# A two-layer hybrid trunk on one core: key weights split in small buffers, values of linear attention kept in SBUF, other orders of additions, loads and first steps

## The chip, the cores and the metric

The kernel runs on one core of one Trainium2 chip. The metric is device time in microseconds (us) of one execution. Engines are named as in the profile: PE (TensorE, matrix products), DVE (VectorE), ACT (ScalarE), POOL (GpSimd), and SP, which issues all DMAs.

## The reference

The input is 1024 positions of width 1024 in float32. Two layers follow, each a token mixer and an MLP, with an RMSNorm ahead of every part and the input added to its output. Layer 0 mixes with dilated attention, which the change leaves alone. Layer 1 mixes with gated linear attention: four heads, keys of 128, values of 256, in chunks of 64 positions. Cut to what matters:

```python
proj = h @ w_in                               # q, k, v, g_out, gate_lr
gk = gate_lr @ w_gate_up + b_gate
log_a = log_sigmoid(gk) / 16.0
b = cumsum(log_a)                             # within a chunk
q_t, k_t = q * exp(b), k * exp(-b)
o_intra = (causal(q_t @ k_t.T)) @ v
U = (k * exp(b_last - b)).T @ v               # state is a * state + U
o = o_intra + q_t @ s_prev
o = rmsnorm(o, norm_w) * silu(g_out)
x = x + o @ w_out
a = relu(h @ w_up)                            # the MLP of each layer
x = x + (a * a) @ w_down
```

## The kernel before, in words

All engines run in an order written out by the program: what Python calls first stands first in an engine's queue, and nothing is reordered. Large products are made with fp32r, three passes for a product of full precision (high by high, high by low, low by high), so every operand is first cut on ACT into a high part and subtracted on DVE to get the low part. They use a scheme of seven block products for eight, so weights and results are also added and subtracted on DVE.

**The MLP of layer 0** (`Up.run`, L786) goes over 16 column pairs p, each of seven products s of 12 matmuls. ACT copies a bank of PSUM to a small tile e (`copy`, L719), DVE adds another bank to it (`done`, L726, and `add`, L747), ACT squares, and SP stores. Beside it, for p from 4 on, runs `Ahead` (L527): it splits the weights of the linear attention's queries and keys (`w_in`, four heads), to be stored and fetched again later. A step of it, at each odd s, issues first the subtractions left over from the step before, then its own cuts: `load` brings four blocks in two tiles, the step after cuts two of them, and five more follow. Pairs of high and low tiles come from the ring k4 (25 tiles of 512 KB).

**The keys' stage** (`finish_keys`, L435) makes queries and keys from these weights, again by seven products a head, with banks X, V, Y, Z; sums of them (L1781) go out to memory as qks. Work of the gates (`Gate`, L1827: logits, log sigmoid, a scan over positions, exponentials, four products that scale queries and keys, a store) is entered in an agenda by clock, and `advance` runs what is due after each product.

**The gate products** (`Values`, L833) make silu's input and the values: 28 steps n of 24 matmuls, two column groups g. `step` (L954) first copies or adds the banks that are complete (`sums`, L933), then makes the operands for step n+2 (`total`, L865; `rounded`, L887; `remain`, L895, with dl at L898), loads for n+5, and issues the product; `advance` comes after it, with `Silu` (L1902) and the late gates. Both groups are stored in memory: silu's input as zscr, the values as uscr.

**The linear attention** (`Pair`, L1964) runs after the last step, two heads at a time. `load_keys` and `wide` load the keys, the gates (G) and the values (V) back; `scores` (L1993) makes masked scores AM; `turn` transposes keys through a bank and ACT copies them (L2008); `update` (L2010) adds to the state Sb; `output` (L2027) makes pO, ACT squares it into gj (L2037); `scaled`, one tick later, takes the root (L208 to L214) and multiplies by G into y (L2045). The first three blocks of the first pair run before the output projection, the rest, as a list of steps, between the products of that projection (`add_block`, L192 to L194), whose weights are prepared by `Weights` (L134 load, L148 high part on ACT, L149 low part on DVE), called raw, whi and wlo.

Rings of tiles: h8 (12), k4 (25), t2 (8 tiles of 256 KB), r6 (1); PSUM has eight banks, taken in turn. A new tile waits until the tile that last had its place is no longer read.

Of the kernel before, what the change touches and what calls it, by code (L numbers as in the profile page):

```python
# [41 lines left out]
def hybrid_trunk(ctx, tc, x, norm_mix, norm_mlp, norm_fin, a_in, a_out, g_in, g_up, g_b, g_nw,  # L42
# [68 lines left out]
    class Weights:  # L111
        def __init__(self):
            self.slots = []
            self.scales = []
            self.ndma = 0
            self.nprep = 0
            self.used = 0
            self.freed = 0
            self.limit = 5
            self.second = pool  # L120
            self.parts = {}
            self.raws = {}
# [29 lines left out]
        def pump(self):  # L152
            while self.ndma < min(self.nprep + RAW, len(self.slots)):
# [107 lines left out]
    class Halves:  # L261
# [173 lines left out]
        def finish_keys(self, low_rank):  # L435
# [8 lines left out]
            def go(p, s):  # L444
                up.product(p, s)
                advance()

            go(0, P1)
# [5 lines left out]
            up.fetch(0, "b")  # L454
# [5 lines left out]
            up.fetch(1, "b")  # L460
# [9 lines left out]
            go(3, P2)  # L470
            up.add(2, P2)
# [3 lines left out]
            up.fetch(0, "g", "d")  # L475
            go(0, P6)
            self.sum3()
# [3 lines left out]
            up.fetch(1, "g", "d")  # L481
# [3 lines left out]
            up.fetch(2, "b")  # L485
            go(1, P5)
            go(0, P7)
# [4 lines left out]
            up.fetch(2, "g", "d")  # L492
# [4 lines left out]
            up.fetch(3, "b")  # L497
# [3 lines left out]
            up.done(2, P6)  # L501
            go(2, P5)
            go(0, P3)
            up.add(0, P3)
            up.fetch(3, "g", "d")
# [100 lines left out]

    def up_columns(i):
# [12 lines left out]
    class Up:  # L620
# [4 lines left out]
        def __init__(self, i):  # L625
# [5 lines left out]
            self.side = Ahead(key_columns, raw_k4, wpre[2]) if i == 0 else None  # L631
# [154 lines left out]
        def run(self, tail):  # L786
# [7 lines left out]
            for p in range(3, NP):  # L794
                first = 2 if p == 3 else 0
                for s in range(first, 7):
# [13 lines left out]
                    if self.side is not None and 4 <= p < NP - 1 and s % 2:  # L810
                        self.side.step()
# [147 lines left out]


# [516 lines left out]
    def out_proj(layer, wbc_row, o, up):  # L1477
# [26 lines left out]
        for tb in range(NB):  # L1504
# [3 lines left out]
            if tb == (NB - 4 if layer else 3):  # L1508
                W.limit = 6
            for n in range(2):  # L1510
# [316 lines left out]
    class Gate:  # L1827
# [10 lines left out]
        def first(self):  # L1838
            z = logits(self.h, self.half) if self.z is None else self.z
            b = bgate[:, self.h:self.h + 1]  # L1840
            a = self.a = t2([P, 512], F32, "ga")
            m = self.m = t2([P, 512], F32, "gmn")
# [35 lines left out]
        def keys(self):  # L1878
            bs = lambda t: t.rearrange("p (b s) -> p b s", s=P)
            d = [self.d[:, c, :].unsqueeze(2).to_broadcast([P, 4, CH]) for c in range(2)]  # L1880
            mm, sk = k4([P, 2, 512], F32, "qkm"), k4([P, 2, 512], F32, "qsk")
            q, k, eq, ek, es = (bs(t) for t in (self.qk[:, 0, :], self.qk[:, 1, :], self.eb[:, 0, :], self.eb[:, 1, :],
                                                self.es))
            q_m, k_m, q_s, kd = (bs(t[:, i, :]) for t in (mm, sk) for i in range(2))
            dve.scalar_tensor_tensor(q_m, q, DK ** -0.5, eq, op0=OP.mult, op1=OP.mult)
            pool.tensor_tensor(q_s[:, :, CH:], q_m[:, :, CH:], d[0], op=OP.mult)
            dve.tensor_tensor(k_m, k, ek, op=OP.mult)
            to = gks[self.h][:, :, 512 * self.half:512 * self.half + 512]
            sp.dma_start(to[:, 0:2, :], mm)
            dve.scalar_tensor_tensor(q_s[:, :, :CH], q[:, :, :CH], DK ** -0.5, es[:, :, :CH], op0=OP.mult, op1=OP.mult)  # L1890
            dve.tensor_tensor(kd[:, :, CH:], k[:, :, CH:], es[:, :, CH:], op=OP.mult)
            dve.tensor_tensor(kd[:, :, :CH], k_m[:, :, :CH], d[1], op=OP.mult)
            sp.dma_start(to[:, 2:4, :], sk)

        def plan(self, t, gap):
# [4 lines left out]
            at(t + 3 * gap - (gap > 1), self.keys, 8)  # L1900

    class Silu:  # L1902
# [19 lines left out]
        def third(self):  # L1922
# [4 lines left out]
            sp.dma_start(self.at(gscr), e)  # L1927

        def plan(self, t):
            for n, (fn, rank) in enumerate(((self.load, 9), (self.first, 8), (self.second, 8), (self.third, 8))):  # L1930
                at(t + n + (n > 0), fn, rank)

    gates = Values(g_in, [2048, 1024], lambda g: (zscr, uscr)[g])
    gates.h = keys.h
    c = clock[0]
    zg = {}

    def early_logits(h, half):
        if h not in zg:
            zg[h] = k4([P, S], F32, "zg")  # L1940
        act.activation(zg[h][:, 512 * half:512 * half + 512], logits(h, half), AF.Copy)

    def late_gate(h, half, t):
        def fn():
            Gate(h, half, zg[h][:, 512 * half:512 * half + 512]).plan(t, 1)
        at(t - 1, fn)

    for n, (h, half) in enumerate(((0, 1), (1, 1), (0, 0), (1, 0))):
        Gate(h, half).plan(c + 15 + 3 * n, 2)
    for n, (h, half) in enumerate(((2, 1), (3, 1), (2, 0), (3, 0))):  # L1950
        at(c + 25 + n // 2, lambda h=h, half=half: early_logits(h, half), 9)
        late_gate(h, half, c + 30 + 2 * n)
    for n in range(5):
        at(c + 17 + n, lambda n=n: gates.load(n), 9)
    at(c + 22, lambda: gates.prep(0), 9)
    at(c + 25, lambda: gates.prep(1), 9)
    halves.finish_keys(low_rank)
    c = clock[0]
    for n, (i, q) in enumerate(((0, 0), (1, 0), (0, 1), (2, 0), (3, 0), (1, 1), (2, 1), (3, 1))):
        Silu(i, q).plan(c + (7, 9, 13, 15, 17, 19, 21, 23)[n])  # L1960

    AM = [k4([P, NB, P], F32, "AM") for _ in range(2)]

    class Pair:  # L1964


        def __init__(self, h0):
            self.h0 = h0
            self.st = {}
            self.y = {}  # L1970
            self.Sb = [None, None]

        def load_keys(self):
            self.q_m, self.k_m, self.q_s, self.kT = [[k4([P, NB, P], F32, n) for _ in range(2)]
                                                     for n in ("q_m", "k_m", "q_s", "kT")]
            for i, ts in ((0, self.k_m), (1, self.q_m)):
                for j in range(2):
                    sp.dma_start(ts[j], gks[self.h0 + j][:, 1 - i, :].rearrange("p (b s) -> p b s", s=P))
            for i, ts in ((3, self.kT), (2, self.q_s)):
# [3 lines left out]
        def wide(self, name, src, half):  # L1983
            ts = getattr(self, name, None)
            if ts is None:
                ts = [h8([P, NB, DV], F32, name) for _ in range(2)]
                setattr(self, name, ts)
            for j in range(2):
                c = DV * (self.h0 + j)
                sp.dma_start(ts[j][:, 4 * half:4 * half + 4, :],  # L1990
                             src[512 * half:512 * half + 512, c:c + DV].rearrange("(b p) c -> p b c", p=P))
# [18 lines left out]
        def update(self, b):  # L2010
            if b == NB - 1:
                return
            ps = bank("pU").rearrange("p (i d) -> p i d", i=2)
            for i in range(2):
                pe.matmul(ps[:, i, :], self.kd[i][:, b, :], self.V[i][:, b, :], start=True, stop=True)  # L2015
            if b % 4 == 0:
                self.Sb = [k4([P, 4, DV], F32, "Sb") for _ in range(2)]
            for i in range(2):
                new = self.Sb[i][:, b % 4, :]
# [7 lines left out]
        def output(self, b):  # L2027
            po = bank("pO").rearrange("p (i d) -> p i d", i=2)
            ss = sm([P, 2], "gss")
            for i in range(2):  # L2030
                if b:
                    pe.matmul(po[:, i, :], self.q_s[i][:, b, :], self.st.pop((b, i)), start=True, stop=False,  # L2032
                              skip_group_check=True)
                pe.matmul(po[:, i, :], AM[i][:, b, :], self.V[i][:, b, :], start=b == 0, stop=True,  # L2034
                          skip_group_check=True)
                junk = t2([P, DV], F32, "gj")
                act.activation(junk, po[:, i, :], AF.Square, accum_out=ss[:, i:i + 1])  # L2037
# [148 lines left out]
```

## Time and profile before

| what | value |
|---|---|
| median of 3 runs | 2707.7 us (2706.05 to 2709.4) |
| profiled execution, its time | 2707.54 us |
| its span | 2705.8 us |
| PE busy | 2609.8 us |
| DVE busy | 1877.5 us |
| ACT busy | 1281.4 us |
| bytes moved | 536.43 MB |

The span runs from the first to the last instruction on the core; 1.7 us of the time lie around it. A row of the time line gives start, length, engine, line, operation, names out<-in, and in brackets the idle time of the engine before it with what ended it. "PEclk" in a window is the mean clock that PE was granted, as a share of full. Matmuls overlap, so the length of one is more than the distance to the next.

### The profile page before, as it was taken

To read this page: it belongs to the slowest core of one execution; us is meant where nothing else is said; L and a number is where in the kernel's file an instruction comes from. 1 tells how busy PE (TensorE), PEld (TensorE's weight loads), DVE (VectorE), ACT (ScalarE), POOL (GpSimd) and SP (SyncE) were. 2 spreads that over 40 slices of the span, in tenths; PEclk is the share of its full clock that TensorE was granted. 3 is DMA by queue.
4 is the path that set the end of the run, shared out by engine and by line. 5 is a ranking of instruction groups with operands and counts; after the bars stand their busy time and mean duration, and the time that the engine had idled before them with its cause. 6 is when DMAs were issued, how large, how long until landed. Compare 5 with 4: busy or idle time off the path is not lost. (4 is left out here: it accounts for less than half of the span.)

```text
span 2705.8 us, 33577 instructions
## 1 busy us (share of the span) xinstructions
PE 2609.8 (96%) x12096; PEld 2159.5 (80%) x12096; DVE 1877.5 (69%) x3002; ACT 1281.4 (47%) x2344; POOL 34.7 (1%) x40
## 2 busy tenths in 40 slices
PE   8999999999999999898999999999689999999998
PEld 6888888888888887776888888777578888888887
DVE  7766788888888565666668775677455666656567
ACT  6443455555555354454544443454234555453344
POOL 0000000000000000000000000310000000000000
PEclk9999999999999999999999999999899999999999
DMA  5775456556556557666788755777534644486543
GB/s 183 247 269 175 124 140 161 144 146 165 135 153 196 181 198 251 203 218 210 271 299 304 257 204 187 256 246 237 217 109 156 242 158 145 152 315 214 191 146 126
DMA packets 355832, 536.43 MB, mean 198 GB/s; under 512 B 23408, under 2 KB 187632, under 8 KB 355664
## 3 DMA queue, kind: packets, MB, share of 16 engines
q1 hardware_dynamic: 355664, 534.27, 60.4%
q8 instruction: 95, 1.56, 0.2%
q14 instruction: 73, 0.60, 0.1%
HBM read 335.29 MB, written 173.74 MB: 188 GB/s over the span
## 5 line engine op out<-in xcount | busy, mean ns | idle before, releaser
L1607 PE MATMUL pB<-dh 128*128 128x512 f32 x512 | 199.2, 389 | 0.0
L1607 PE MATMUL pB<-dl,dh 128*128 128x512 f32 x512 | 199.2, 389 | 0.0
L1607 PE MATMUL pB<-dh,dl 128*128 128x512 f32 x512 | 199.2, 389 | 0.0
L201 DVE TENSOR_TENSOR dl<-sin,dh 128x1024 fp32r<-128x1024 f32 x112 | 136.7, 1221 | 65.6 <-ACT dh L198 62.6
L714 PE MATMUL pV<-s4h,wd 128*128 128x512 f32 x480 | 165.7, 408 | 13.4 <-DVE rb L739 8.6
L198 ACT ACTIVATE dh<-sin 128x1024 fp32r<-128x1024 f32 x112 | 117.8, 1052 | 80.6 <-PE pB L1607 26.7
L1021 ACT ACTIVATE pt<-pt,orow 128x128 f32<-128x128 f32 (+1 forms) x192 | 85.0, 443 | 146.4 <-DVE orow L1019 144.4
L1607 PE MATMUL pA<-dh 128*128 128x512 f32 x384 | 149.6, 389 | 0.0
L1607 PE MATMUL pA<-dh,dl 128*128 128x512 f32 x384 | 149.4, 389 | 0.0
L1607 PE MATMUL pA<-dl,dh 128*128 128x512 f32 x384 | 149.4, 389 | 0.0
L198 ACT ACTIVATE dh<-kept 128x1024 fp32r<-128x1024 f32 x64 | 67.8, 1060 | 146.2 <-DVE kept L1572 105.2
L714 PEld LDWEIGHTS pV<-s4h,wd 128*128 128x128 f32 x480 | 92.8, 193 | 34.9 <-DVE rb L739 9.5
L1607 PEld LDWEIGHTS pB<-dl,dh 128*128 128x128 f32 x512 | 96.1, 188 | 20.0
L1607 PEld LDWEIGHTS pB<-dh 128*128 128x128 f32 x512 | 96.1, 188 | 19.9
L1607 PEld LDWEIGHTS pB<-dh,dl 128*128 128x128 f32 x512 | 96.1, 188 | 19.9
L719 ACT ACTIVATE e<-pX 128x512 f32<-128x512 f32 x108 | 63.6, 589 | 101.1 <-PE pX L714 101.1
L714 PE MATMUL pX<-s2h,wbh 128*128 128x512 f32 x240 | 97.7, 407 | 9.8 <-ACT e L719 9.8
L714 PE MATMUL pX<-s3h,wgh 128*128 128x512 f32 x240 | 98.6, 411 | 7.9 <-ACT e L719 7.9
L652 DVE TENSOR_TENSOR wbl<-t,wbh 128x1024 fp32r<-128x1024 f32 x48 | 58.8, 1225 | 66.8 <-ACT wbh L651 66.8
L723 ACT ACTIVATE c<-c 128x512 f32<-128x512 f32 x64 | 40.4, 631 | 123.4 <-DVE c L751 73.5
L652 DVE TENSOR_TENSOR wal<-raw,wah 128x512 fp32r<-128x512 f32 x96 | 65.9, 687 | 44.8 <-ACT wah L651 44.8
L714 PE MATMUL pX<-a11h,wah 128*128 128x512 f32 x240 | 95.9, 399 | 0.0
(321 smaller groups left out, 7436.8 us busy)
## 6 DMA issues: line engine op xcount, KB each, us to landing
sin<-acts SPq DMA_DIRECT2D x112, 512.0 KB, 4.6
acts<-s SPq DMA_DIRECT2D x64, 512.0 KB, 3.5
raw<-in_mlp_w_down_dram SPq DMA_DIRECT2D x64, 512.0 KB, 5.0
raw<-in_attn_w_in_dram SPq DMA_DIRECT2D x96, 256.0 KB, 4.4
cw<-c SPq DMA_DIRECT2D x192, 128.0 KB, 2.3
raw<-in_mlp_w_up_dram SPq DMA_DIRECT2D x48, 512.0 KB, 6.0
acts<-c SPq DMA_DIRECT2D x64, 256.0 KB, 2.2
kept<-in_mlp_w_down_dram SPq DMA_DIRECT2D x32, 512.0 KB, 6.7
```

What stands on the lines that cost most here:

```text
L198: act.activation(hi, src, AF.Copy)
L201: dve.tensor_tensor(lo, src, hi.bitcast(F32), op=OP.subtract)
L652: self.remain(lambda: dve.tensor_tensor(lo, src, hi.bitcast(F32), op=OP.subtract))
L714: pe.matmul(st[b], u[:, k, :], v, start=first and k + n == 0, stop=k == 3 and n == 2, skip_group_check=True)
L719: act.activation(e, self.st[p]["X"], AF.Copy)
L723: act.activation(r, r, AF.Relu)
L1021: act.activation(pt[:, i, :128 * n], pt[:, i, :128 * n], AF.Exp, scale=-1.0, bias=m, accum_out=self.row[:, r, HD:HD + 1])
L1607: pe.matmul(self.acc[s][t], a[:, k, c], b[:, k, :], start=fresh and m + k + v == 0, stop=m == 7 and k == 1 and v == 2, skip_group_check=True)
```

## The change

There are four parts. **Small buffers:** `Trickle` takes the place of `Ahead`. It cuts one block into a pair of small tiles th and tl (ring t2) at a time, and stores each by itself, so that 14 stores of half the size stand for 7. Its raw blocks lie in the tile of r6 and one of t2. A step without work stands behind the load, and the steps come where p + s is even. **Keys:** the agenda is run ahead of a product, not behind it; fetches of split weights stand at other products; a gate's two tiles are one of k4, its four products are made in place on DVE alone, and their store comes one clock later. All late gates take their logits in the gate stage, not from a copy. **Gate products:** `Gates.paced` makes the total of step n+2 first, then the sums, then the high part, then runs the agenda, then makes the low part and the product. **Linear attention:** values are added straight into four SBUF tiles V; uscr and its loads are gone. Keys and gates are loaded, and scores, turn and the first block run, by the agenda between the steps 19 to 27; the last product is in two halves with a block behind each. The root is taken behind each block's output, the rest of the scaling (`flush`) behind the next block's update. The output weights' raw loads begin at steps 24 and 25 of the agenda, and later ones wait until the last block of the projection's first round.

```diff
-                    if self.side is not None and 4 <= p < NP - 1 and s % 2:
+                    if self.side is not None and 4 <= p < NP - 1 and (p + s) % 2 == 0:
                         self.side.step()
...
+            def load():
+                t = wk.tile([P, 3, 4, DK], F32, name="traw", tag="r6", bufs=1)
+                x = t2([P, 4, DK], F32, "traw1")
...
+            def cut(src, hi, lo, i, j):
+                h, l = t2([P, 4, DK], F32R, "th"), t2([P, 4, DK], F32R, "tl")
+                act.activation(h, r[src], AF.Copy)
+                def rest():
+                    dve.tensor_tensor(l, r[src], h.bitcast(F32), op=OP.subtract)
+                    for t, n, k in ((h, hi, i), (l, lo, j)):
+                        sp.dma_start(...)
+                self.behind.append(rest)
...
+            self.todo.extend((load, lambda: None,
+                              lambda: cut("b11", "ah", "al", 0, 0),
+                              lambda: cut("b21", "ah", "al", 1, 1),
+                              lambda: cut("b22", "d", "d", 0, 1),
+                              three, four, five, lambda: cut("b21", "gh", "gl", 1, 1)))
...
             def go(p, s):
+                advance()
                 up.product(p, s)
-                advance()
...
+        def paced(self, n, between, blocks=range(4)):
+            self.load(n + 5)
+            ahead = n + 2 < self.STEPS
+            if ahead and n + 2 not in self.t:
+                self.total(n + 2)
+            self.sums(n)
+            if ahead:
+                self.rounded(n + 2)
+            between()
+            if ahead:
+                self.remain(n + 2)
+            self.product(n, blocks)
...
+            half, quad = divmod({"c11": 0, "c12": 1, "c21": 2, "c22": 3}[name], 2)
+            if (quad, half) not in self.V:
+                self.V[quad, half] = h8([P, 4, 512], F32, "V")
+            dve.tensor_tensor(self.V[quad, half][:, t, :], self.acc[s][t], c, op=OP.add)
...
         def step(self, b):
-            self.output(b)
-            self.update(b + 1) if b + 1 < NB else None
+            po, ss = self.output(b)
+            self.update(b + 1)
+            self.flush()
+            self.open = b, po, self.root(ss)
...
+    for t, fn in ((19, lambda: one.load_keys(("k_m", "q_m", "kT"), Pair.joined)),
+                  (20, lambda: one.load_keys(("q_s",), Pair.apart)),
+                  (20, clear_scores),
+                  (22, lambda: one.load_gates(0)),
+                  (23, lambda: one.load_gates(1)),
+                  (23, out_weights),
+                  (24, lambda: (W.dma(), W.dma())),
+                  (25, lambda: (W.dma(), W.dma())),
+                  (24, lambda: one.scores(0)),
+                  (25, lambda: (one.turn(0), one.scores(1))),
+                  (26, lambda: one.turn(1)),
+                  (27, begin)):
+        at(c + t, fn, 9)
+    for n in range(gates.STEPS - 1):
+        gates.paced(n, advance)
...
+    for p in range(2):
+        blocks = [2 * p, 2 * p + 1]
+        if p == 0:
+            gates.paced(last, advance, blocks)
+        else:
+            gates.product(last, blocks)
+        for t in blocks:
+            gates.add("c21", "B", t, 1)
+        one.step(p + 1)
+        W.prep(dve)
```

More of the change, by code (lines that the diff above doesn't have):

```diff
@@ L1950, in hybrid_trunk @@
[L1950 to L1952 removed]
+        Gate(h, half).plan(c + 16 + 3 * n, 2)
     for n in range(5):
[L1954 to L1956 removed]
+        at(c + 18 + n, lambda n=n: gates.load(n), 9)
+    at(c + 23, lambda: gates.prep(0), 9)
+    at(c + 26, lambda: gates.prep(1), 9)
@@ L2078, in hybrid_trunk, with clear_scores, out_weights @@
-    for t in range(4):
-        gates.add("c21", "B", t, 1)
-    keys.h.clear()
-    one.wide("V", uscr, 1)
-    ol = []
-    W.second = dve
-    W.limit = 2
-    one.start()
-    tick()
-    for b in range(3):
-        one.step(b)
-        tick()
+    def clear_scores():
+        for _ in range(2):
+            t = k4([P, NB, P], F32, "AM")
+            pool.memset(t, 0.0)
+            AM.append(t)
+    def out_weights():
+        for k in range(0, KT, 2):
+            add_rows(g_out, k, gnw)
```

251 lines of the change are left out of this document (134 added, 117 removed).

## Prediction

> **What bounds the kernel now.** I read the busy times of the engines first, then what PE waited for, then the stretches that the change touches, each as one window. Times are microseconds; a difference of 0.2% (5.4 us) is about what a measurement of this kernel can tell from no change.
>
> ```profile
> PE 2609.8 (96%) x12096; PEld 2159.5 (80%) x12096; DVE 1877.5 (69%) x3002; ACT 1281.4 (47%) x2344; POOL 34.7 (1%) x40
> ```
>
> PE is the bound, and neither the number of its products nor their shapes change, so the time can only move by what PE loses to waits and to a lower clock. The waits of PE, by what they waited for (sum, times, longest):
>
> ```profile
> PE pX L714 <- ACT e L719: 17.7, 14, 3.6
> PE pO L2034 <- ACT gj L2037: 15.0, 2, 14.4
> PE pO L2032 <- ACT gj L2037: 11.7, 14, 1.7
> PE pV L714 <- DVE rb L739: 8.6, 2, 5.9
> PE pB L913 <- DVE c L928: 5.1, 1, 5.1
> PE pV L714 <- DVE qk L1781: 3.7, 2, 3.0
> PE pA L1998 <- DVE c L928: 2.9, 1, 2.9
> ```
>
> All seven lie in stages that the change rewrites. The windows put sizes to them. The first is ten column pairs of layer 0's MLP beside the splitting of the keys' weights, the second the same ten of layer 1, without it; then come the keys, the gate products, and linear attention's start and rest. The columns are length, busy PE (count), PEld, DVE, ACT, POOL, PEclk, DMA share, GB/s.
>
> ```profile
> 1056.18:1284.39 228.21, 204.07 (x841) 162.50 (x840) 145.50 (x214) 113.13 (x169) 0.00 (x0) 0.96 0.62 210
> 2160.01:2350.41 190.40, 190.40 (x841) 157.50 (x840) 119.68 (x171) 96.76 (x140) 0.00 (x0) 1.00 0.47 155
> 1630.00:1730.00 100.00, 93.78 (x418) 75.56 (x418) 59.74 (x99) 47.60 (x89) 14.04 (x15) 0.98 0.66 234
> 1790.00:1830.00 40.00, 34.86 (x142) 28.31 (x141) 32.93 (x38) 18.08 (x22) 0.94 (x1) 0.91 0.77 266
> 1888.00:1928.00 40.00, 19.95 (x100) 16.37 (x99) 17.24 (x39) 9.61 (x28) 0.00 (x0) 0.79 0.82 313
> 1928.00:2045.00 117.00, 103.85 (x473) 82.78 (x474) 59.79 (x153) 32.64 (x104) 0.00 (x0) 0.96 0.31 103
> ```
>
> The same 841 matmuls take 37.8 longer in layer 0. One matmul there comes every 190.40/841 = 0.226, a product of 12 every 2.72, a gate step of 24 every 5.43. For the others, idle time plus the share below full clock: keys 6.2 + 2.0 = 8.2; gates 5.1 + 3.6 = 8.7; start 20.1 plus some 3.4 of half clock while PE worked (an estimate: much of the lower clock fell on idle time) = 23.5; rest 13.2 + 4.7 = 17.9. In all 96.
>
> **Splitting the keys' weights.** The work stays: 28 cuts on ACT, 28 subtractions and 16 differences on DVE. Its place changes; here is ACT in that stage, where th, ah and gh are cuts and e the copy that a later product waits for. Before:
>
> ```order
> L719 ACTIVATE e_10000<-pX 128x512
> L651 ACTIVATE wbh<-t 128x1024
> L719 ACTIVATE e_10042<-pX 128x512
> L651 ACTIVATE wgh<-t 128x1024
> L560 ACTIVATE ah<-praw 128x512 x2
> L723 ACTIVATE rb<-rb 128x1024
> ```
>
> Now:
>
> ```order
> L705 ACTIVATE wah<-raw 128x512
> L629 ACTIVATE th<-traw_10469 128x512
> L773 ACTIVATE e_10623<-pX 128x512
> L705 ACTIVATE wah<-raw 128x512
> L777 ACTIVATE c_10639<-c_10639 128x512
> L778 ACTIVATE c_10639<-c_10639 128x512
> L629 ACTIVATE th<-traw 128x512
> L773 ACTIVATE e_10666<-pX 128x512
> ```
>
> The two cuts in a row, one step behind their load, become single cuts, each in front of an e, with an empty step behind the load. What the load costs now, and what a clean column pair leaves of room:
>
> ```profile
> 1117.67 2.69 SPq L548 DMA_DIRECT2D praw<-in_gla_w_in_dram  x4
> 1122.14 0.63 ACT L560 ACTIVATE ah<-praw 128x512 fp32r<-128x512 f32 x1 [2.62 <-DMA praw<-in_gla_w_in_dram]
> 1125.12 0.63 ACT L560 ACTIVATE ah<-praw 128x512 fp32r<-128x512 f32 x1 [2.35 <-DMA praw<-in_gla_w_in_dram]
> 1131.39 0.58 ACT L719 ACTIVATE e<-pX 128x512 f32<-128x512 f32 x1
> 1132.02 0.79 PE L714 MATMUL pX<-s2h,wbh 128*128 128x512 f32 x1 [3.62 <-ACT e L719]
> 1288.76 0.58 ACT L719 ACTIVATE e<-pX 128x512 f32<-128x512 f32 x1
> 1289.83 0.39 PE L714 MATMUL pX<-s2h,wbh 128*128 128x512 f32 x1
> ```
>
> ACT stood 2.62 + 2.35 before two cuts, all behind them slid, and PE waited 3.62. The four places with the largest such waits, as windows:
>
> ```profile
> 1072.00:1084.00 12.00, 9.28 (x34) 7.16 (x33) 5.01 (x7) 6.83 (x10) 0.00 (x0) 0.86 0.49 169
> 1128.00:1140.00 12.00, 8.38 (x26) 6.38 (x25) 8.24 (x14) 6.31 (x11) 0.00 (x0) 0.72 0.57 177
> 1195.00:1207.00 12.00, 10.05 (x37) 7.78 (x36) 8.58 (x14) 6.60 (x11) 0.00 (x0) 0.86 0.65 223
> 1231.00:1247.00 16.00, 10.11 (x33) 7.87 (x32) 5.71 (x9) 8.35 (x13) 0.00 (x0) 0.79 0.55 191
> ```
>
> In 52 us they hold 130 matmuls where 230 fit (52/0.226): 100 x 0.226 = 22.6 lost, waits and half clock together. The load landed 1125.12 - 1117.67 = 7.45 after its issue; the empty step makes its room four products, 10.9, so I take the 22.6 as gone. The other 15.2 are the cuts' own 28 places, 0.54 each, and stay: the clean pair has 1289.83 - (1288.76 + 0.58) = 0.49 between e and the product that needs it, so a 0.63 cut ahead of e shows with 0.14, and shows more where a subtraction or two differences (0.69 each on DVE) stand in the same chain. The new places are at products 0, 2, 4 and 6 of even pairs too, which were free of this; I take 0.65 for each, 18 in all (bounds: 8, if half of the places stay hidden; 37.8, if all is as now). Gain 20, from 0 to 30.
>
> **The keys' stage.** Gate work that stood ahead of the additions on DVE now stands behind them, and the split weights are fetched at other products, the first ones earlier. What the old order cost:
>
> ```profile
> 1719.04 1.22 DVE L1859 TENSOR_TENSOR_SCAN ga<-gc,gmn 128x512 f32<-128x512 f32 x1
> 1723.63 0.68 DVE L1781 TENSOR_TENSOR qk<-pV,e 128x512 f32<-128x512 f32 x1
> ```
>
> The addition that frees pV sat behind the scan and five key products, 1719.04 to 1723.63, for a PE wait of 3.0. That goes. POOL's product moves to DVE, at no more than the 0.68 of a row as wide as the addition's, and the stores move one clock on; both now run behind the addition, which covers them unless DVE's queue reaches the next one, 5.4 later. Of 8.2 I leave 3.5 (1 to 7) for small waits and cuts: gain 5.
>
> **The gate products.** The 5.1 wait is the addition behind silu and keys on DVE:
>
> ```profile
> 1793.06 1.22 DVE L1924 TENSOR_TENSOR gd<-gd,ge 128x1024 f32<-128x1024 f32 x1
> 1800.01 1.27 DVE L928 TENSOR_TENSOR c<-pB,c 128x512 f32<-128x512 f32 x2
> ```
>
> 6.95 of work of the agenda lay between. Now additions come ahead of the agenda, but the remainder dl comes behind it, and PE needs dl two steps later. Where the agenda holds the same 6.95 and dl's own 1.23, that is 8.2 of the 10.9 of two steps, so most fits; three places where a late gate's ACT chain or a bank for its logits comes in I put at 0.9, 2.6 and 0.9: 4.5 left (0 to 9), gain 4.
>
> **Linear attention.** Before, ACT's whi waited for a load queued on SP behind the stores of the values, and the squares gj behind it held PE:
>
> ```profile
> 1893.50 5.98 SPq L931 DMA_DIRECT2D uscr<-c  x6
> 1905.89 3.42 SPq L134 DMA_DIRECT2D raw<-in_gla_w_out_dram  x6
> 1912.30 2.35 ACT L148 ACTIVATE whi<-raw,masks 128x1024 fp32r<-128x1024 f32 x2 [11.22 <-DMA raw<-in_gla_w_out_dram]
> 1915.15 1.19 PE L2034 MATMUL pO<-V,AM 128*128 128x256 f32 x2 [14.45 <-ACT gj L2037]
> 1892.29 3.37 PE L1998 MATMUL pA<-q_m,k_m 128*128 128x128 f32 x16 [2.89 <-DVE c L928]
> ```
>
> The values' stores and loads are gone and the raw loads are issued among the last steps, so I take the 14.45 and the 2.89 as gone. What is late next is DVE: the scores now come inside the last steps, and take banks that its additions free. On DVE before (c are values, AM the masked scores):
>
> ```order
> L898 TENSOR_TENSOR dl<-raw,dh 128x1024
> L928 TENSOR_TENSOR c_15571<-pA,c_15571 128x512 x2
> L1924 TENSOR_TENSOR gd<-gd,ge 128x1024
> L1925 SCALAR_TENSOR_TENSOR ge<-gd,ge 128x1024
> L1926 SCALAR_TENSOR_TENSOR ge<-gz,ge 128x1024
> L928 TENSOR_TENSOR c_15611<-pA,c_15611 128x512 x2
> L928 TENSOR_TENSOR c_15829<-pB,c_15829 128x512
> L928 TENSOR_TENSOR c_15833<-pB,c_15833 128x512
> L928 TENSOR_TENSOR c_15869<-pB,c_15869 128x512
> L928 TENSOR_TENSOR c_15873<-pB,c_15873 128x512
> L1999 COPY_PREDICATED AM<-masks,pA 128x512 x4
> ```
>
> Now (V are values):
>
> ```order
> L922 TENSOR_TENSOR raw<-raw,kept 128x1024
> L2016 TENSOR_TENSOR V<-pB,c_15683 128x512
> L2016 TENSOR_TENSOR V<-pB,c_15685 128x512
> L1993 TENSOR_TENSOR gd<-gd,ge 128x1024
> L1994 SCALAR_TENSOR_TENSOR ge<-gd,ge 128x1024
> L1995 SCALAR_TENSOR_TENSOR ge<-gz,ge 128x1024
> L2074 COPY_PREDICATED AM<-masks,pA 128x512 x2
> L952 TENSOR_TENSOR dl<-raw,dh 128x1024
> L922 TENSOR_TENSOR raw<-raw,kept 128x1024
> L2016 TENSOR_TENSOR V<-pB,c_15724 128x512
> L2016 TENSOR_TENSOR V<-pB,c_15726 128x512
> L1984 TENSOR_SCALAR gd<-gd 128x1024
> ```
>
> The masked copies wait for PE's scores in the middle of the queue, and dl, the next total and the next values stand behind them. From step 22 to step 24's additions DVE has one silu end (3 x 1.23), two dl (2.46), two totals (2.4), a silu start (0.68) and the additions (1.27): 10.5 with widths as in the rows above, and some 5.8 of waiting for ACT's copies and exponentials between them (an estimate): 16.3 against two steps of PE, 10.9. So the first scores wait 5.4 (0 to 6), half clock takes 3.4 after it, the next step up to 2.3, the scaling of block 0 ahead of a bank's release 2.9 and the out weights' cuts ahead of a gj 2.9, with 4 in small waits: 21 of the start's 23.5 come back. In the rest, each of the steps waits for gj as at
>
> ```profile
> 1957.75 0.70 PE L2032 MATMUL pO<-Sb,q_s 128*128 128x256 f32 x2 [0.83 <-ACT gj L2037]
> ```
>
> and root and power no longer stand ahead of gj; the second set of raw loads and the keys in two portions move ahead of it. I leave 0.6 for each of 12 steps and one cut of 2 or so, 9 of 17.9 (6 to 18). Gain 2.5 + 9 = 11.5.
>
> The Trainium skill ("TensorE: Matmul & The Clock Gate", Part 1) gives half rate after an idle window of about 3.4 us; by it the 5.4 costs a half-rate stretch and the shorter waits none, where my sum has 3.4 in one. The trace is harder than that: in the window at 1195.00 the mean clock is 0.86 though PE waited less than 2 us there.
>
> **Rivals.** (1) The new places hide. For it: DVE and ACT are busy 145.50 and 113.13 of 228.21 there, so there is room beside the chain of e; against: the room in that chain is 0.49. Then the MLP keeps 8 and the start 7: 2667 - 10 - 14 = 2643. (2) DVE falls back at two steps, not one, so that the scores stall twice, or whi waits for raw again: 5.4 + 3.4 + half of 14.45 = 16 more: 2683. For it: the queue above, in which the copies wait for PE and PE for the additions; against: the raw loads no longer follow six stores. (3) The loads were not the cause in the MLP: the cuts' places are, and 37.8 stays: 2667 + 20 = 2687. For it: fourteen waits on e, four large; against: the 2.62 and 2.35 above. (4) Slower: th and tl are in a ring of eight small tiles with e and c; each is held until its store lands, and a late one stops ACT or DVE. The nearest rows for a store:
>
> ```profile
> acts<-c SPq DMA_DIRECT2D x64, 256.0 KB, 2.2
> wp_ah<-ah SPq DMA_DIRECT2D x12, 512.0 KB, 5.6
> ```
>
> At 2.2 the ring turns without waiting, at 5.6 it does not. A stall like that at 1128.00 costs 12 - 26 x 0.226 = 6.1; beyond eight of 28 steps the gain of 40 is gone, and at eleven the time is 2667 + 67 = 2734. The Trainium skill ("DMA: Bandwidth & Descriptors", Anatomy of one DMA) has a fixed cost of about 2.0 us for every DMA, so 14 half stores would hold tiles as long as 7 whole ones each; the 2.2 agrees.
>
> **How the numbers follow.** 20 + 5 + 4 + 11.5 = 40.5. The profiled execution took 2707.54, the median is 2707.7: 2667. Chances: forecast 0.45, rival (1) 0.20, (2) 0.15, (3) 0.12, (4) 0.08. The range leaves out (4) and the faster half of (1), and takes in the bounds of keys and gates: 2640 to 2692. Faster is all but (4) and a part, 0.03, where (2) and (3) meet near 2703: 0.89, 0.03, 0.08.
>
> **What would show it.** In the MLP's window no cut waits on DMA, and the length for 841 matmuls falls to some 208; if it stays at 228, rival (3). The addition after the scan's place comes before it. At the first scores a wait of some 5 on an addition; if it is absent, rival (1); a wait of whi for raw, rival (2). Waits on t2 stores of th or tl behind ACT or DVE: rival (4). A stall in a stage that the change leaves alone, or PE's busy time at another count, would make the whole sum wrong.

## The result and the profile after

The changed kernel takes 2679.5 us (median of 4 runs, 2678.4 to 2679.8), the kernel before 2708.6 beside it: a ratio of 0.9892, with a 95% interval of 0.9875 to 0.9909. That is 29 us less, where 40.5 were forecast. The profiled execution took 2679.75, its span is 2678.0. One execution below, the profiled one of the kernel with its first steps after the products, took 5493 us with a product every 0.467 where 0.227 is usual; it is left out, so that kernel has a time and no profile.

Waits of PE after the change, in the stages that it rewrites (sum, times, longest), to be held against the seven lines of before:

```profile
PE pX L768 <- ACT e L773: 15.1, 13, 2.6
PE pO L2107 <- ACT gj L2111: 11.6, 14, 2.5
PE pA L2073 <- DVE V L2016: 10.5, 2, 10.2
PE pB L967 <- DVE dl L952: 3.5, 4, 2.2
PE pV L768 <- DVE rb L793: 1.5, 2, 1.0
PE pT L239 <- DVE gy L2133: 2.0, 1, 2.0
PE pV L768 <- DVE qk L1849: 0.2, 1, 0.2
```

Gone are the 14.4 of pO on gj, most of the 8.6 on rb, the 5.1 on c and the 3.7 on qk. New are one wait of 10.2, the first scores on the additions of values, and smaller ones on dl (3.5) and on gy (2.0), the scaling of block 0. The 10.2 is the wait that the prediction called late next, at nearly twice its forecast size.

The same stretches as windows (length, busy PE, PEld, DVE, ACT, POOL with counts, PEclk, DMA share, GB/s): ten column pairs of layer 0's MLP, the keys, the first 22 gate steps, and linear attention from step 22 to the first product of the output projection.

```profile
1076.09:1291.07 214.98, 198.03 (x841) 157.15 (x840) 145.94 (x214) 111.80 (x168) 0.64 (x2) 0.99 0.63 212
1610.00:1710.00 100.00, 99.42 (x453) 81.14 (x452) 65.83 (x111) 47.01 (x90) 12.35 (x12) 1.00 0.64 232
1707.90:1834.70 126.80, 123.61 (x532) 100.42 (x531) 98.13 (x131) 63.59 (x98) 16.06 (x14) 0.99 0.71 239
1834.70:1905.96 71.26, 53.70 (x249) 43.79 (x248) 45.82 (x65) 30.77 (x56) 0.00 (x0) 0.92 0.54 195
```

Before, the last two were:

```profile
1728.80:1856.60 127.80, 122.66 (x530) 100.99 (x529) 95.66 (x121) 61.51 (x93) 19.80 (x19) 0.97 0.65 218
1856.60:1927.89 71.29, 51.24 (x238) 42.18 (x236) 41.66 (x62) 25.67 (x48) 0.00 (x0) 0.88 0.82 290
```

The MLP's pairs went from 228.21 to 214.98: 13.2. The ten pairs of after begin one pair later, because the changed splitting reaches one pair further; all eleven together went from 247.3 to 234.2, which gives 13.1. Idle time and the share below full clock in the keys' window went from 8.2 to 0.6: 7.6. The gate steps went from 127.80 to 126.80, with two matmuls more: 1.0. In the six kernels below that leave these steps as changed, the same 22 steps took 126.8 to 128.5 in their profiled executions, so the 1.0 cannot be told from nothing. From step 22 to the first product of the projection nothing changed in length, 71.29 and 71.26, though the new stretch holds one block more. From there to the same product of the next MLP it took 207.6 before (1927.89 to 2135.53) and takes 201.3 (1905.96 to 2107.24): 6.4. The sum is 28.2, and the two profiled executions differ by 2707.54 - 2679.75 = 27.8.

Where the 10.2 comes from, on DVE, on ACT and on PE (start, length, engine, line, operation, out<-in, and in brackets the idle time before with its releaser):

```profile
1844.77 1.23 DVE L1993 TENSOR_TENSOR gd<-gd,ge 128x1024 f32<-128x1024 f32 x1 [5.08 <-ACT ge L1989]
...
1848.43 1.22 DVE L952 TENSOR_TENSOR dl<-kept,dh 128x1024 fp32r<-128x1024 f32 x1
1849.57 1.22 DVE L922 TENSOR_TENSOR kept<-kept 128x1024 f32<-128x1024 f32 x1
1852.91 0.69 DVE L1984 TENSOR_SCALAR gd<-gd 128x1024 f32<-128x1024 f32 x1 [2.13 <-ACT gd L1983]
1853.52 1.22 DVE L952 TENSOR_TENSOR dl<-kept,dh 128x1024 fp32r<-128x1024 f32 x1
1854.66 1.22 DVE L922 TENSOR_TENSOR raw<-raw,kept 128x1024 f32<-128x1024 f32 x1
1855.79 1.28 DVE L2016 TENSOR_TENSOR V<-pB,c 128x512 f32<-128x512 f32 x2
```

```profile
1842.58 1.06 ACT L1988 ACTIVATE ge<-gd 128x1024 f32<-128x1024 f32 x1 [1.74 <-DMA gscr<-ge]
1850.88 1.06 ACT L946 ACTIVATE dh<-kept 128x1024 fp32r<-128x1024 f32 x1 [5.17 <-DVE kept L922]
```

```profile
1835.39 0.50 PE L967 MATMUL pB<-dl,s4h 128*128 128x512 f32 x1 [0.29 <-DVE dl L952]
1856.53 3.79 PE L2073 MATMUL pA<-qq_m,qk_m 128*128 128x128 f32 x16 [10.18 <-DVE V L2016]
```

DVE is not busy all the time: it stood 5.08 and 2.13 for ACT, and ACT stood 5.17 for DVE. Total, copy, exponentials, silu's end and dl pass back and forth between the two engines, and 1.74 of it is a tile still being stored. The chain is late before the scores: at 1835.39 PE, one product into step 22, waits 0.29 for dl of that same step, which the program orders ahead of the product of step 20. The additions end at 1857.07, 22.4 after step 22 began at 1834.70, where the prediction had 16.3.

### The profile page after: what moved, and what is told of

It is laid out like the page before. It is cut to its first block, busy times and chain, and to the rows that moved or that the text cites. A ratio compares the mean times of both kernels' runs of the same rounds, so it can differ in the third digit from the quotient of the medians.

```text
span 2678.0 us, 33562 instructions
## 1 busy us (share of the span) xinstructions
PE 2600.7 (97%) x12096; PEld 2151.9 (80%) x12096; DVE 1881.7 (70%) x3010; ACT 1279.6 (48%) x2340; POOL 29.3 (1%) x32
## 4 chain that ended last, share of the span: by engine, by line
PE 74%; DVE 11%; ACT 6%; DMA 4%; issue 4%; SPq 0%; DVEq 0%; ACTq 0%
PE pB L1675 13%; PE pX L768 12%; PE pA L1675 10%; PE pV L768 8%; PE pB L967 6%; PE pY L768 4%; PE pA L967 4%; PE pZ L768 4%; PE pd L194 2%; PE pd L195 2%; PE pd L193 2%; PE pS L1072 1%; PE pO L1113 1%; DMA cw<-c 1%; DVE c L1166 1%
## 5 line engine op out<-in xcount | busy, mean ns | idle before, releaser
L768 PE MATMUL pY<-a12h,wah 128*128 128x512 f32 x240 | 96.0, 400 | 0.0
```

Of the source, the lines that this page charges most:

```text
L768: pe.matmul(st[b], u[:, k, :], v, start=first and k + n == 0, stop=k == 3 and n == 2, skip_group_check=True)
```

## The experiments

Two theories were set against each other for the linear attention: that the first scores wait because DVE is short of time in the last steps, and that the order of the queues makes one chain of two engines. For the MLP the question was whether loads or the cuts' places make the loss. Times are medians; each ratio is to the kernel before, measured beside it.

| kernel | us | ratio to before, 95% interval |
|---|---|---|
| changed, old splitting | 2693.0 | 0.9944, 0.9927 to 0.9961 |
| before, new splitting | 2696.1 | 0.9955, 0.9940 to 0.9970 |
| changed, scores one step later | 2677.4 | 0.9886, 0.9871 to 0.9900 |
| changed, two silus in the projection | 2684.9 | 0.9916, 0.9901 to 0.9930 |
| changed, dl ahead of the agenda | 2669.0 | 0.9856, 0.9842 to 0.9871 |
| changed, total one step earlier | 2669.6 | 0.9859, 0.9843 to 0.9876 |
| changed, splitting at products 3 to 5 | 2684.4 | 0.9912, 0.9898 to 0.9927 |
| changed, small tiles at the old places | 2685.1 | 0.9916, 0.9901 to 0.9930 |
| changed, total and dl ahead | 2665.8 | 0.9847, 0.9831 to 0.9864 |
| changed, differences earlier | 2679.2 | 0.9898, 0.9883 to 0.9912 |
| changed, first steps after the products | 2677.9 | 0.9890, 0.9874 to 0.9907 |
| changed, keys' agenda behind the product | 2679.0 | 0.9905, 0.9888 to 0.9923 |

**The old splitting in the changed kernel.**

```diff
-            self.side = Trickle(wpre[2]) if i == 0 else None
+            self.side = Ahead(key_columns, raw_k4, wpre[2]) if i == 0 else None
...
-                    if self.side is not None and 4 <= p < NP - 1 and (p + s) % 2 == 0:
+                    if self.side is not None and 4 <= p < NP - 1 and s % 2:
```

> The changed kernel with the old splitting of the keys' weights in layer 0's MLP (pairs of large tiles, steps at odd products, no empty step behind the load); everything else as changed. Theory (a load that lands after ACT asks for it, and the half clock behind the wait, were 22.6 us of the old loss of 37.8, and the new places give some of it back): the ten column pairs of the MLP go from 214.98 to about 228, ACT waits for praw come back, time 2679.5 + 13 = 2692.5 (2689 to 2696). Rival (the part is worth what it was only beside other changes): less than 2685.

It took 13.5 more. Its window of the ten pairs, and the cuts that waited for their load:

```profile
1057.19:1285.19 228.00, 202.81 (x842) 161.53 (x840) 145.45 (x214) 113.19 (x169) 0.00 (x0) 0.96 0.62 210
```

```profile
1073.39 0.63 ACT L561 ACTIVATE ah<-praw 128x512 fp32r<-128x512 f32 x1 [4.39 <-DMA praw<-in_gla_w_in_dram]
1124.21 0.63 ACT L561 ACTIVATE ah<-praw 128x512 fp32r<-128x512 f32 x1 [3.28 <-DMA praw<-in_gla_w_in_dram]
1234.31 0.63 ACT L561 ACTIVATE ah<-praw 128x512 fp32r<-128x512 f32 x1 [6.91 <-DMA praw<-in_gla_w_in_dram]
```

228.00 is the 228.21 of before again, with the waits on the load: six of them, 18.1 in sum (18.3 in the kernel before).

**The new splitting in the kernel before.** `Trickle` and its steps were added to the kernel before in place of `Ahead`, nothing else.

> The kernel before with only the new splitting of the keys' weights. Theory (the parts add up, since each lies in a stretch of its own): 2708 - 13 = 2695 (2691 to 2698), no cut in the MLP waits on a DMA, and about 24 us of waits for e stay. Rival (the new split needs the room that the other parts make in the rings): above 2703.

```profile
1074.88:1290.62 215.74, 198.25 (x841) 157.15 (x840) 145.85 (x214) 111.81 (x168) 0.64 (x2) 0.99 0.63 211
```

215.74 for the ten pairs, and 12 us less in all. This part adds to the others, and is worth 12 to 13.5. Not every wait on a load went, though: one cut in four heads still waits, 1.67 here and 1.54 in the changed kernel:

```profile
1181.59 0.63 ACT L629 ACTIVATE th<-traw 128x512 fp32r<-128x512 f32 x1 [1.54 <-DMA traw<-in_gla_w_in_dram]
```

**Scores one step later.**

```diff
-                  (24, lambda: one.scores(0)),
-                  (25, lambda: (one.turn(0), one.scores(1))),
-                  (26, lambda: one.turn(1)),
+                  (25, lambda: one.scores(0)),
+                  (26, lambda: (one.turn(0), one.scores(1))),
+                  (27, lambda: one.turn(1)),
```

> The changed kernel with scores(0), turn(0) with scores(1), and turn(1) entered one step later (25, 26, 27 in place of 24, 25, 26). Theory (the 10.2 us wait of the first scores is for two banks that step 24's additions free, at the end of a queue on DVE and not for want of DVE time): product 24 runs in that gap, the wait falls below 3, time 2679.5 - 8 = 2671.5 (2668 to 2675). Rival (DVE is short of time in the last steps): PE waits about as long one product later, for dl or for the same scores, time 2677 to 2682.

The 10.2 is gone, but only 2 us are won:

```profile
1852.85 0.50 PE L967 MATMUL pA<-dl,s3h 128*128 128x512 f32 x1 [1.87 <-DVE dl L952]
1859.68 2.05 PE L2073 MATMUL pA<-qq_m,qk_m 128*128 128x128 f32 x16 [1.31 <-DVE V L2016]
1868.98 1.25 PE L2082 MATMUL pk<-ident,qkT 128*128 128x128 f32 x8 [1.79 <-DVE V L2016]
1871.79 2.05 PE L2073 MATMUL pA<-qq_m,qk_m 128*128 128x128 f32 x16 [1.55 <-DVE AM L2074]
```

The wait fell into four, 6.5 in sum, on dl, values and AM. The rival's time came true: the scores only met first what was late already. Whether DVE lacks time there or stands in a chain with ACT, this run does not tell.

**Two silus in the projection.** The pieces of steps 21 and 23, which the second pair of heads reads, were loaded, worked and stored between blocks 4 and 7 of the first pair.

> The changed kernel with the last two of the eight silu pieces, which only the second pair of heads reads, taken out of steps 21 to 26 and put into the steps of the output projection. Theory of DVE time (the first scores wait because 8.8 us of silu work on DVE and 6.3 us on ACT stand in those steps): the wait of 10.2 falls to 3 or less, the projection takes the work in its idle time, time 2679.5 - 8 = 2671.5 (2667 to 2675). Theory of the queue order (the piece at step 19 with its store is what the scores' additions stand behind): the wait falls by less than 3, time 2677 to 2682, or more if ACT's exponentials stand ahead of gj in the projection.

```profile
1856.90 3.78 PE L2073 MATMUL pA<-qq_m,qk_m 128*128 128x128 f32 x16 [6.72 <-DVE V L2016]
1926.55 0.97 PE L2107 MATMUL pO<-Sb,qq_s 128*128 128x256 f32 x2 [3.71 <-ACT gj L2111]
```

With two pieces less the wait fell by 3.5, to 6.7: more than the one theory said and less than the other. The time is one that the theory of the queue order allowed. From step 22 to the projection it took 67.1, 4.1 less than the changed kernel; the projection took 9.4 more, in part because the exponentials stood ahead of gj on ACT, as in the second line. So taking work away helps some, but this run takes it from DVE and ACT alike and does not separate work from order. The next three leave the work as it is and change its order alone.

**dl ahead of the agenda.**

```diff
             if ahead:
                 self.rounded(n + 2)
-            between()
-            if ahead:
                 self.remain(n + 2)
+            between()
             self.product(n, blocks)
```

> The changed kernel with the low part dl of step n+2 made ahead of the agenda again, not behind it. Theory of the round trip (in each gate step total on DVE, the copy dh and the exponentials on ACT, silu's end and dl on DVE stand in one chain, about 1.22 + 1.06 + 2.1 + 3.7 + 1.22 = 9.3 in a step with a silu's end and 5.2 in one with a silu's start, 14.5 for two steps of PE that take 10.9, so DVE falls back 3.6 every two steps from step 13 on; with dl ahead, it lies beside the exponentials and the chain is 12.3): the scores' wait of 10.2 falls to 2 to 5, time 2679.5 - 6 = 2673.5 (2670 to 2676). Rival (the wait is DVE's sheer work): the wait stays at 8 or more, 2678 to 2682.

**The total one step earlier.** This adds, behind `self.sums(n)`, the total of step n+3.

```diff
             self.sums(n)
+            if n + 3 < self.STEPS and n + 3 not in self.t:
+                self.total(n + 3)
             if ahead:
                 self.rounded(n + 2)
             between()
```

> The changed kernel with the total of step n+3 made in step n, behind the additions and ahead of the agenda; dl stays behind the agenda. Theory of the round trip (the copy dh no longer waits for a total that stands behind silu's end; what is left is DVE's own work of some 10.5 for two steps, less than 10.9): the scores' wait falls below 4, time 2679.5 - 7 = 2672.5 (2669 to 2676). Rival (DVE's sheer work): 2678 to 2682, the wait moves by a step.

**Both.** Here dl of step n+2 and then the total of step n+3 stand ahead of the agenda.

> The changed kernel with both: dl of step n+2 ahead of the agenda, and the total of step n+3 as well. Theory of the round trip (each of the two alone took the scores' wait from 10.2 to 6.5 and 4.5; with both, only DVE's sheer work of 10.5 in two steps is left): wait of 3 or less, 2665 (2662 to 2668). Rival (what is left of the wait is DVE's sheer work and the additions' place behind it): wait as in the better of the two, 2668 to 2671.

The scores in the three kernels, with dl ahead, with the total earlier and with both:

```profile
1847.48 3.78 PE L2072 MATMUL pA<-qq_m,qk_m 128*128 128x128 f32 x16 [6.47 <-DVE V L2015]
```

```profile
1846.77 3.78 PE L2075 MATMUL pA<-qq_m,qk_m 128*128 128x128 f32 x16 [4.47 <-DVE V L2018]
```

```profile
1844.33 3.78 PE L2074 MATMUL pA<-qq_m,qk_m 128*128 128x128 f32 x16 [3.91 <-DVE V L2017]
```

And the first 22 gate steps of the one with both:

```profile
1708.90:1829.40 120.50, 120.50 (x533) 99.65 (x532) 100.17 (x133) 64.19 (x99) 13.00 (x14) 1.00 0.76 259
```

PE now stands nowhere in 22 steps, where the changed kernel lost 126.80 - 120.50 = 6.3, though DVE does as much work (100.17 to 98.13). Each kernel breaks the chain at another link, each is 10 us faster than the changed one, both together 13.7. That order, and not the amount of work, made the lag is shown for the gate steps, and for 6.3 of the 10.2 at the scores. What holds the 3.9 that stay was not tried. All three waits came out above what was expected: 6.5 for 2 to 5, 4.5 for less than 4, 3.9 for 3 or less. The first two times were still 4.5 and 2.9 below their forecasts, since these counted the scores' wait alone and not the gate steps before it, which gave 5.3 and 4.7; the third was 0.8 above. This last kernel is the fastest of the study, 41.5 us below the kernel before.

**The first steps after the products.** Scores, turn and the first block were taken out of the agenda and put behind the last product.

> The changed kernel with scores, turn and the first block run behind the last gate product, as before the change, not between the last products; all else as changed (values in SBUF, loads and weights early). Theory (the interleaving itself loses what it was worth to the first scores' bank wait, 10.2 and the half clock behind it; run behind, the products 24 to 27 wait only for dl, and some 6 come back as waits of the chain scores, AM, kd, Sb): 2676 to 2681. Rival (the interleaving hides the chain of scores, kd and the first state, and is worth more than its wait): 2684 to 2690. Second rival (the wait only cost): 2672 or less.

1.6 us less than the changed kernel, within what can be told. As the queues stand in the changed kernel, the interleaving itself is worth nothing. It may give back at the scores' banks what it hides, but no profile of this kernel shows it. With dl and the total ahead it was not tried.

**The splitting at products 3, 4 and 5.**

```diff
-                    if self.side is not None and 4 <= p < NP - 1 and (p + s) % 2 == 0:
+                    if self.side is not None and (3 <= p < NP - 1 and 3 <= s <= 5 and (p, s) not in ((3, 3), (3, 4))):
```

The load of a head goes with the last cut of the one before, with an empty step behind it.

> The changed kernel with the splitting's steps at products 3, 4 and 5 of each column pair alone, the load of a head sent with the last cut of the head before, an empty step behind it. Theory of places (the 24.6 us that are left are cuts and differences ahead of e1 and e2, at products 0, 1, 2 and 6; behind e2 ACT has 2.2 us of room ahead of e3 and 1.9 ahead of the squares, and DVE 1.2 ahead of e3's addition): the ten pairs fall from 214.98 to 197 or so, time 2679.5 - 17 = 2662.5 (2658 to 2668). Rival (the work of ACT and DVE is too much wherever it stands): losses move to e3's addition rb and the product pV, 2675 to 2682.

```profile
PE pV L771 <- DVE rb L796: 13.6, 7, 2.7
PE pX L771 <- ACT e L776: 3.1, 2, 1.9
```

```profile
1116.71 0.60 ACT L776 ACTIVATE e<-pX 128x512 f32<-128x512 f32 x1 [5.18 <-DMA wp_gh<-th]
```

My theory of places fell. The waits on e went from 15.1 to 3.1, but 13.6 came up on rb. Steps in a row also use the ring of small tiles faster than the stores empty it: e waited 5.18 for the store of a th. This is rival 4 of the prediction, in a kernel that asks for it.

**Small tiles at the old places.** Steps at odd products, no empty step.

```diff
-                    if self.side is not None and 4 <= p < NP - 1 and (p + s) % 2 == 0:
+                    if self.side is not None and 4 <= p < NP - 1 and s % 2:
...
-            self.todo.extend((load, lambda: None,
+            self.todo.extend((load,
```

> The changed kernel with the small tiles kept, but with the steps at odd products as before and no empty step behind the load. Theory of the load (the empty step and the single cuts removed the waits, not the size of the tiles): ACT waits for traw again, one or two cuts for each of four loads, time 2679.5 + 8 = 2687.5 (2684 to 2693). Rival (smaller tiles and stores did it): no waits on the load, 2674 to 2681.

```profile
1073.72 0.63 ACT L629 ACTIVATE th<-traw 128x512 fp32r<-128x512 f32 x1 [4.06 <-DMA traw<-in_gla_w_in_dram]
1186.34 0.63 ACT L629 ACTIVATE th<-traw 128x512 fp32r<-128x512 f32 x1 [3.28 <-DMA traw<-in_gla_w_in_dram]
1251.24 0.63 ACT L629 ACTIVATE th<-traw 128x512 fp32r<-128x512 f32 x1 [5.48 <-DMA traw<-in_gla_w_in_dram]
```

5.6 us slower than the changed kernel, with three cuts that wait for the load, 12.8 in sum. But it is also 7.9 faster than the kernel with the old splitting, where six waits sum to 18.1. Over the eleven pairs the three take 247.1 with the old splitting, 241.9 here and 234.2 as changed. So the empty step and the spacing are worth 6 to 8, and the single cuts in small tiles 5 to 8, at the old places and without the empty step. Both theories hold in part; through what the single cuts help, beyond fewer waits on the load, was not tried apart.

**The differences earlier.** Each head's four differences were put behind the cut of the step before.

```diff
+            def two():
+                cut("b22", "d", "d", 0, 1)
+                less("b11", "b12", "b11")
+                less("b12", "b22", "b12")
+
             def three():
-                less("b11", "b12", "b11")
-                less("b12", "b22", "b12")
                 cut("b11", "bh", "bl", 1, 1)
+                less("b22", "b22", "b11")
```

> The changed kernel with the four differences of each head's blocks made one step of the splitting earlier, so that no cut waits for a difference made in its own step. Theory (of the 24.6 us lost in the ten column pairs, most is e behind a cut that waits for DVE's differences, 1.96 in the example at 1146.15; there are 12 such cuts): 214.98 falls to 206, time 2679.5 - 9 = 2670.5 (2667 to 2674). Rival (any cut ahead of e costs its 0.6, and DVE's differences cost the same wherever they stand): 2677 to 2681.

```profile
1075.12:1291.18 216.06, 199.07 (x841) 158.50 (x840) 146.08 (x214) 111.31 (x168) 0.64 (x2) 0.98 0.63 211
```

No gain: 216.06 where the changed kernel has 214.98. The time is the rival's.

**The keys' agenda behind the product.** The two lines of `go` were put back in their old order.

> The changed kernel with the keys' stage in its old order of product and agenda (the gate work ahead of the additions on DVE again); the new places of the fetches, the in-place products and the later stores stay. Theory (an addition that frees pV stood behind the scan and five key products, and PE waited up to 3.0 and fell to half clock): some 4 to 5 come back in the keys' stage, time 2684 (2681 to 2687). Rival (the fetches' places or the in-place products gave what the stage gained): 2678 to 2681.

```profile
1610.00:1710.00 100.00, 98.43 (x447) 79.97 (x446) 64.11 (x107) 45.74 (x88) 12.37 (x12) 1.00 0.64 232
```

Idle time in the keys' window is 1.6 in place of 0.6, and the total is the same. The order that I held to be the cause gives 1 of 7.6. The trace of before shows what else held the addition at 1723.63. It also needs e, and ACT made e late:

```profile
1720.29 0.73 ACT L1854 ACTIVATE eb<-ga 128x256 f32<-128x256 f32 x2 [2.42 <-DVE ga L1859]
1721.23 1.06 ACT L1941 ACTIVATE zg<-pg 128x512 f32<-128x512 f32 x2
1722.19 0.59 ACT L719 ACTIVATE e<-pX 128x512 f32<-128x512 f32 x1
```

e ended at 1722.78, behind exponentials that had waited 2.42 for the scan and behind copies zg of the late gates' logits, which neither the changed kernel nor this one makes. So the five products on DVE held that addition for 0.85 at most, and here, in the old order without zg, PE waits 0.79 and 0.39 for additions of this kind. That leaves the fetches, the clock of the gates' plan, the four products in place and the logits of the late gates with their copies, which were not tried apart: what freed this stage stays open.

## Why the prediction was right, and where its terms were not

The time lies in the range and the direction holds; the sum was 11.5 too large, and rival 2's 2683 lies nearer to 2679.5 than the forecast's 2667. Three of the four terms were too large and one too small, so their errors cancel in part, which is luck. By its steps:

- **The splitting:** forecast 20, measured 13.2 by the windows, 13.5 and 12 by the two kernels that move this part alone. The mechanism was right in the main: ACT's waits on loads fall from 18.3 to 1.5, and the mean clock rises from 0.96 to 0.99. "I take the 22.6 as gone" holds but for that one wait. The step that failed is "I take 0.65 for each, 18 in all": what stays is 214.98 - 190.40 = 24.6, or 0.88 for each of 28 cuts. Two theories of why, places and differences, fell; the kernels with other places lost as much or more, on e, on rb or on the ring. What the 24.6 consists of stays open.
- **The keys:** forecast 5, measured 7.6. The step "That goes" came true, but its reason, the order of gate work and additions, carries 1 of it. The gain is there by luck, from parts of the change to which the prediction gave no price.
- **The gates:** forecast 4, measured 1.0, or nothing. The step that failed is that dl behind the agenda costs 8.2 of the 10.9 of two steps, "so most fits". It counted work on DVE alone; with ACT's copies and exponentials between, the chain comes to 14.5 (the estimate of the expectation above), longer than PE's 10.9, and the lag grows. The kernel with dl ahead again shows it: its 22 steps take 121.5.
- **Linear attention:** forecast 11.5, measured 6.4 (7.5 to 9.1 in the profiled executions of the five kernels that leave this stage and the gate steps as changed). The 14.45 and the 2.89 went, as said, and the first scores became late, as said. The term that failed is "the first scores wait 5.4 (0 to 6)": 10.2. It started DVE's chain at step 22 as if it were on time there, and it was already late; and it did not have the 1.74 for a tile under store. The half clock behind the wait was put too high, at 3.4: the first 16 products of scores take 3.79, the next 16 take 2.05, so it cost 1.7. Step 22 to the first product of the projection has the same length as before, with block 3 in it, which stood before inside the projection. In the projection the wait of most steps fell from 0.83 to 0.56; a few longer ones came in, up to 2.5, so that the waits on gj sum to 11.6, where they were 11.7:

```profile
1968.52 0.70 PE L2107 MATMUL pO<-Sb,qq_s 128*128 128x256 f32 x2 [0.56 <-ACT gj L2111]
1996.41 0.80 PE L2107 MATMUL pO<-Sb,qq_s 128*128 128x256 f32 x2 [2.01 <-ACT gj L2111]
```

- **The rivals:** rival 2 is nearest to what happened, with its first half, a scores' wait of 10 us, and without its second: whi no longer waited for raw. Rival 1 falls with the 24.6 and the 10.2. Rival 3 is excluded by the fall of 13.2 in the MLP, which the old splitting undoes. Rival 4's condition came true, but without its harm. The nearest row that the prediction had for a store, 2.2, was not what the new ones took:

```profile
wp_ah<-th SPq DMA_DIRECT2D x8, 256.0 KB, 5.7
```

This is as long as the 5.6 of the whole tiles of before. For the Trainium skill's figure ("DMA: Bandwidth & Descriptors", Anatomy of one DMA) the prediction had half stores hold their tiles as long as whole ones. The Trainium skill gives that 2.0 us there for DMAs that GpSimd issues, and SP issues all of these; the measured stores decide. The equal hold came out for ah and bh (4.7 both), not for the low parts, whose halves landed in 2.1 to 3.3 where the whole ones took 3.3 to 4.2. ACT stood behind stores of th:

```profile
1158.63 0.60 ACT L773 ACTIVATE e<-pX 128x512 f32<-128x512 f32 x1 [2.90 <-DMA wp_bh<-th]
```

This is the third copy of a column pair. Another such copy, at 1223.31, waits 3.12, and PE lost next to nothing at either. In a clean pair of the kernel before, ACT stands 2.16 ahead of that copy, which is the room that took these waits:

```profile
1298.24 0.60 ACT L719 ACTIVATE e<-pX 128x512 f32<-128x512 f32 x1 [2.16 <-PE pX L714]
```

## What to carry to other kernels

Where two engines feed a third, write down the chain over a whole period, with every step that stands in front of another only because of its queue, and compare it with the period of the bound engine; a chain of some 14.5 (an estimate) in a period of 10.9 is hidden until its lead is used up, and then shows at the first thing that takes a bank. Remainders that nobody needs at once are not free to move behind other work: put what closes a chain early and what merely fills time late. And where a wait is removed by moving work, measure the part alone, since an order that looks like the cause may give only a small share.

## What was not expected of the hardware

Half the bytes did not always free a tile sooner: the stores of ah and bh landed in medians of 5.7 and 4.7 at 256 KB, and in 5.6 and 4.7 at 512 KB.

The length of a wait of PE did not decide alone whether half clock followed. In the MLP it followed waits of 1.95 (before, at 1197.59) and of 1.87, in the kernel with dl ahead; in the changed kernel PE waits 1.87 before the same product, and the clock stays full. Here is the window of 15 us around that wait, first with dl ahead, then as changed:

```profile
1255.00:1270.00 15.00, 13.13 (x52) 10.35 (x51) 12.50 (x20) 6.02 (x9) 0.00 (x0) 0.89 0.74 245
1255.00:1270.00 15.00, 13.13 (x59) 10.55 (x58) 12.98 (x20) 6.03 (x9) 0.00 (x0) 1.00 0.76 255
```
